# An encoder layer with seven-product weight blocks: two of the four sums of quarters of the weights are added by accumulating transfers

## The chip, the core and the metric

The kernel runs on one core of a Trainium2 chip. The metric is the device time of one execution in microseconds, taken as the median of several runs; a profiled execution gives the trace that the rows below come from. Engines are named as the profile names them: PE (TensorE matmul) and PEld (its weight load), DVE (VectorE), ACT (ScalarE), POOL (GpSimd) and SP (SyncE, which here only issues transfers).

## What is computed

One layer of an encoder on 528 tokens (16 learned ones and 512 of the input) with 1024 features, all in float32. A SwiGLU half-step, a mixer (a gated linear recurrence beside a Fourier mixing), a second SwiGLU half-step and a last norm follow each other. The half-steps are where the change sits:

```python
def swiglu(h, w_in, w_out):
    gate, up = jnp.split(h @ w_in, 2, axis=-1)
    return (jax.nn.silu(gate) * up) @ w_out

h = h + 0.5 * swiglu(rms_norm(h, norm_ffn1[l]), w_ffn1_in[l], w_ffn1_out[l])   # w_in 1024 x 5632, w_out 2816 x 1024
...
h = h + 0.5 * swiglu(rms_norm(h, norm_ffn2[l]), w_ffn2_in[l], w_ffn2_out[l])
return rms_norm(h, norm_final)[:, N_META:]
```

## The kernel before

**Exact parts.** Every float32 operand of a product is split into a rounded part `hi` and a rest `lo`, and a product is three matmuls (hi by hi, hi by lo, lo by hi, in `mm3`). For weights, `split_w` takes the `hi` part on ACT (L87) and the `lo` part on DVE (L88).

**Seven products in place of eight.** The 2816 hidden features are done in 22 blocks of 128. A block needs a gate and an up product over 1024 features. The first blocks of a half-step (4 of the first, 2 of the second) are done plainly; the other 38, here called *pairs* 0 to 37 (0 to 17 in the first half-step, 18 to 37 in the second), treat gate and up as a 2 by 2 matrix of quarters [A11 A12; A21 A22] (rows gate and up, columns the two halves of the features) and the stream, split by features and tokens, likewise, and need seven products of quarters. PE does them in the order p1 (A11), p2 (A12), p6 (S2), p5 (S1), p7 (S3), p3 (S4), p4 (A22). The tiles for that are made in three jobs:

- `pair_blocks`: loads the two raw tiles of 512 KB (`g`, then `u`, L101), splits all of the first (*A*, L87 and L88) and the second half of the second (`jh`, `jl`), then adds in place on DVE: S3 = A11 - A21 (L110), S1 = A21 + A22 (L111), S2 = A22 - S3 (L112).
- `pair_sums`: splits S1 and S2 (*S*, one L87 and one L88 of 1024 columns), then S4 = A12 - S2 (L120).
- `pair_differences`: splits S3 and S4 (*D*).

The stream's side has matching sums (`sums_of_x`), and `pair` puts the seven products together on DVE, multiplies by the norm's roots, takes Silu on ACT and splits the result.

**Order.** Weight jobs stand in one list in the order of their use, and `block` starts a job three jobs ahead of its use (LOOK = 3). Raw tiles share four buffers and split tiles four, so a load waits until an earlier split has read its buffer. A tile scheduler fixes the order on each engine when the program is built; on the chip each engine runs its list strictly in order. With chunks of four blocks (pairs 7 to 17 in the first half-step), each pair is followed on PE by two blocks of the way out (`po`, L462 takes them up). There the load of the tile that is split first waits for the *S* split of the pair before, and the load of the other for its *D* split.

Of the kernel before, what the change touches and what calls it, by code (L numbers as in the profile page):

```python
# [12 lines left out]
ALU = mybir.AluOpType  # L13
# [49 lines left out]
def encoder_layer(ctx: ExitStack, tc: tile.TileContext, xT, vecs, w1i, w1o, wm, wg, wo, w2i, w2o,  # L63
# [13 lines left out]
    def spans(n):  # L77
        """The pieces of n columns that fit in a bank."""
        return [(0, n)] if n <= 512 else [(0, n // 2), (n // 2, n)]
# [5 lines left out]
    # [A11 A12; A21 A22]: rows gate and up, columns the two halves of the features  # L85
# [9 lines left out]

    def pair_blocks(pair):
        """A11, A12 and A22; then, in place, S3 = A11 - A21, S1 = A21 + A22 and S2 = A22 - S3."""
        raw = []
        for src in pair["src"]:
            r = wraw.tile([P, 1024], F32, tag="raw", name="raw")  # L100
            nc.sync.dma_start(r.rearrange("p (k m) -> p k m", m=P), src)  # L101
            raw.append(r)
        pair["raw"] = raw
        hi, lo = w_tiles()
        split_w(hi, lo, raw[0])
        jh = state["pool"].tile([P, 512], F32R, tag="jh", name="jh")
        jl = state["pool"].tile([P, 512], F32R, tag="jl", name="jl")
        split_w(jh, jl, raw[1][:, 512:])
        g, u = raw
        nc.vector.tensor_tensor(g[:, :512], g[:, :512], u[:, :512], op=ALU.subtract)  # L110
        nc.vector.tensor_tensor(u[:, :512], u[:, :512], u[:, 512:], op=ALU.add)  # L111
        nc.vector.tensor_tensor(u[:, 512:], u[:, 512:], g[:, :512], op=ALU.subtract)  # L112
        return [(quarter(hi, 0), quarter(lo, 0)), (quarter(hi, 1), quarter(lo, 1)), (quarter(jh, 0), quarter(jl, 0))]

    def pair_sums(pair):
        """S1 and S2; then, in place, S4 = A12 - S2."""
        g, u = pair["raw"]
        hi, lo = w_tiles()
        split_w(hi, lo, u)
        nc.vector.tensor_tensor(g[:, 512:], g[:, 512:], u[:, 512:], op=ALU.subtract)  # L120
        return [(quarter(hi, 0), quarter(lo, 0)), (quarter(hi, 1), quarter(lo, 1))]

    def pair_differences(pair):
        """S3 and S4."""
        g = pair.pop("raw")[0]
        hi, lo = w_tiles()
        split_w(hi, lo, g)
        return [(quarter(hi, 0), quarter(lo, 0)), (quarter(hi, 1), quarter(lo, 1))]

    def parts_given(src):  # L130
        """Both parts of a table, as they come."""
        parts = []
        for i, t in enumerate(w_tiles()):
            raw = wraw.tile([P, 1024], F32, tag="raw", name="raw")
            t, raw = [x[:, :3 * HT] for x in (t, raw)]
            nc.sync.dma_start(raw.rearrange("p (k m) -> p k m", m=HT), src[i])
            nc.scalar.activation(t, raw, AF.Copy)
            parts.append(t.rearrange("p (k m) -> p k m", m=HT))
        return parts

# [1 line left out]
    # (source, partitions, tiles, columns of a tile, tiles per load) or a part of a pair  # L142
    jobs = []

    def ffn_steps(chunks, late):
        """Blocks of features on their way in, each followed by its share of the preceding chunk's way out."""
        steps, f0, prev = [], 0, None
        for c in chunks:
            for i in range(c):
                steps.append(("in", f0 + i, None))  # L150
                if prev:
                    steps += [("out", prev, d) for d in range(*(max(0, ND - (c - k) * ND // c - late) if k < c else ND for k in (i, i + 1)))]
            prev = (f0, f0 + c)
            f0 += c
        return steps + [("out", prev, d) for d in range(ND)]
# [3 lines left out]
    def ffn_jobs(wi, wo_, steps, classic):  # L159
        for kind, f, d in steps:  # L160
            if kind == "out":
                jobs.append((wo_[d][:, f[0]:f[1], :], P, f[1] - f[0], P, 8))
            elif f in classic:
                for b in range(2):
                    jobs.append((wi[f, b], P, 8, P, 2 if len(jobs) < 3 else 8))
            else:
                pair = {"src": (wi[f, 0], wi[f, 1])}
                for part in (pair_blocks, pair_sums, pair_differences):
                    jobs.append((part, pair))
# [56 lines left out]
    def mm3(outs, wh, wl, xh, xl, first, last):  # L226
        """outs[i] += w.T @ x[i], w and x in two exact parts each."""
        for i, o in enumerate(outs):
            nc.tensor.matmul(o, wh, xh[i], start=first, stop=False)  # L229
        for i, o in enumerate(outs):  # L230
            nc.tensor.matmul(o, wh, xl[i], start=False, stop=False)  # L231
        for i, o in enumerate(outs):
            nc.tensor.matmul(o, wl, xh[i], start=False, stop=last)  # L233

    def halves(t, n):
        """The first n columns of a tile by their pieces."""
        return [t[:, a:b] for a, b in spans(n)]

    def times(out_, ps, r, n):
        """out = ps * r, with ps in banks."""  # L240
# [12 lines left out]
    def vec(name, i=0):  # L253
        return V[:, VOFF[name] + i: VOFF[name] + i + 1]

# [11 lines left out]
    # the tensor engine's clock rises while these run, ahead of the first loads' landing  # L267
# [4 lines left out]
    def split_to(hi, lo, src, scale=None):  # L272
        """hi + lo = src * scale exactly but for float32's own rounding."""
# [13 lines left out]
    # [B11 B12; B21 B22]: rows the two halves of the features, columns those of the tokens.  # L287
    # T1 = B12 - B11, T2 = B22 - T1, T3 = T2 - B11, -T4 = B21 - T2, one tile of the features at a time
    def sums_of_x(g, t0, n, k):
# [6 lines left out]
        nc.vector.scalar_tensor_tensor(t1, a[:, m:], vec(g, k), xg[:, :m], op0=ALU.mult, op1=ALU.subtract)  # L296
        nc.vector.scalar_tensor_tensor(t2, b[:, m:], vec(g, k + 4), t1, op0=ALU.mult, op1=ALU.subtract)
        nc.vector.tensor_tensor(t3, t2, xg[:, :m], op=ALU.subtract)
        nc.vector.scalar_tensor_tensor(t4, b[:, :m], vec(g, k + 4), t2, op0=ALU.mult, op1=ALU.subtract)
# [13 lines left out]
    # 1 / sqrt(mean + eps) of each token: the roots are taken with tokens on partitions, then spread to all partitions  # L313
# [20 lines left out]
    def spread_in(ps, q, m):  # L334
        """ps[:, t] = q of token t on all partitions."""
# [14 lines left out]
    def ffn(X, XT, ss, t0, n, steps, classic, on_done, tail, lead=None):  # L350
        st = {"R": ss} if lead else {}
        half = n // 2
        with tc.tile_pool(name="ffn", bufs=10) as fp, tc.tile_pool(name="ffnt", bufs=2) as ft:
# [19 lines left out]
            def pair(R):  # L373
                """Gate and up of one block of features, from seven products of quarters."""
# [10 lines left out]
                gv, uv = q[:, :2, :half], u[:, :, :half]  # L385
# [21 lines left out]
                nc.scalar.activation(gv, gv, AF.Silu)  # L407
# [58 lines left out]
    # softplus(-lambda) = max(-lambda, 0) + log1p(exp(-|lambda|))  # L466
# [21 lines left out]
    # only sets with the root and without it follow: the root's is at hand when the first norm is due  # L488
    nc.scalar.activation(s2[:, :1], epsc, AF.Sqrt)

# [44 lines left out]
    # [cos W | sin W] of each group  # L535
# [11 lines left out]
    X2, XT2 = [], []  # L547
    ss2 = new_ss()
    with tc.tile_pool(name="mx", bufs=1) as mx, tc.tile_pool(name="mt", bufs=2) as mt:
# [5 lines left out]
        def projecting(t0):  # L555
            """One block of the projection, a tile of the features at a time."""
# [7 lines left out]
        def project():  # L564
            """One block of the projection, with steps of what is under way between its products."""
# [4 lines left out]
        # recurrence inputs: depthwise convolution  # L570
# [42 lines left out]
        # Fourier mixing over the tokens t = 0..T-1: s, d[t] = v[t] + v[t + T/2], v[t] - v[t + T/2] give the even and  # L613
        # the odd outputs; the cosines multiply s[t] + s[T/2 - t] and d[t] - d[T/2 - t], the sines the other two, t = 0..T/4
# [19 lines left out]
        # with r in a = exp(-8 r sp) and t = tanh(4 r sp): sqrt(1 - a^2) = (1 + a) sqrt(t)  # L634
# [3 lines left out]
        def recurrences():  # L638
            """The recurrences in steps, each table of the scalar engine's once."""
# [52 lines left out]
        def features(s):  # L692
            """Step s of the token tiles: their transform over the features, tokens on partitions."""
# [34 lines left out]
        def tokens(s, A, py):  # L728
            """Step s of the sum over the tokens."""
# [90 lines left out]
    def tail(acts, ft):  # L820
# [15 lines left out]
        def residual(d0, d1, t0, t1, ps, sq):  # L836
            """The stream's last values, their squares, and the values times the last norm's gain."""
# [4 lines left out]
        def group(t0, t1, between):  # L842
            """The stream's last values for a group of tokens, and the roots of their mean squares."""
# [49 lines left out]
        def finishing(q, t0, t1, queues):  # L893
            """The steps from the roots to the end of a group."""
# [99 lines left out]
```

## Time and profile before

| | us |
|---|---|
| median of 3 runs (lowest to highest) | 883.19 (883.08 to 883.46) |
| span of the profiled execution, first to last instruction | 880.1 |
| difference of the two | 3.1 |
| PE busy in the span | 867.3 |
| DVE busy | 751.8 |
| ACT busy | 423.8 |
| POOL busy | 0.2 |

The span is what the trace shows; the 3.1 us are what the runs' median has beside it. A busy time is the union of an engine's instructions. An engine at 99% can still not be made faster by work taken from another, and one at 85% can still be waited for, so what counts is who waits where.

### The profile page before, as it was taken

To read this page: it belongs to the slowest core of one execution; us is meant where nothing else is said; L and a number is where in the kernel's file an instruction comes from. 1 tells how busy PE (TensorE), PEld (TensorE's weight loads), DVE (VectorE), ACT (ScalarE), POOL (GpSimd) and SP (SyncE) were. 2 spreads that over 40 slices of the span, in tenths; PEclk is the share of its full clock that TensorE was granted. 3 is DMA by queue.
4 is the path that set the end of the run, shared out by engine and by line. 5 is a ranking of instruction groups with operands and counts; after the bars stand their busy time and mean duration, and the time that the engine had idled before them with its cause. 6 is when DMAs were issued, how large, how long until landed. Compare 5 with 4: busy or idle time off the path is not lost.

```text
span 880.1 us, 15868 instructions
## 1 busy us (share of the span) xinstructions
PE 867.3 (99%) x6410; PEld 826.8 (94%) x6410; DVE 751.8 (85%) x1280; ACT 423.8 (48%) x625; POOL 0.2 (0%) x4
## 2 busy tenths in 40 slices
PE   9999999999999999999999999999999999999996
PEld 8999999999999999999887888999899999999996
DVE  7999987898898896867998689999999888789864
ACT  7644433344344343667837555444444444334354
POOL 0000000000000000000000000000000000000000
PEclk9999999999999999999999999999999999999998
DMA  7423333324323223423412331223343324323312
GB/s 236 149 64 112 86 108 96 96 73 122 95 90 118 83 85 109 147 67 107 135 47 96 93 99 48 85 85 120 98 131 81 115 79 120 112 73 101 99 54 96
DMA packets 33497, 88.15 MB, mean 100 GB/s; under 512 B 3728, under 2 KB 7568, under 8 KB 33424
## 3 DMA queue, kind: packets, MB, share of 16 engines
q1 hardware_dynamic: 32880, 86.62, 32.4%
q8 instruction: 50, 0.82, 0.4%
q10 hardware_dynamic: 544, 0.52, 0.2%
q14 instruction: 23, 0.19, 0.1%
HBM read 85.03 MB, written 2.10 MB: 99 GB/s over the span
## 4 chain that ended last, share of the span: by engine, by line
PE 93%; DVE 4%; ACT 1%; DMA 0%; issue 0%; SPq 0%; DVEq 0%
PE pp L229 15%; PE pp L233 15%; PE pp L231 14%; PE po L233 9%; PE po L231 9%; PE po L229 9%; PE pw L231 2%; PE pw L233 2%; PE pm L229 2%; PE pm L233 2%; PE pm L231 2%; PE pw L229 2%; PE pu L229 1%; PE pu L231 1%; PE pu L233 1%; PE pg L229 1%
## 5 line engine op out<-in xcount | busy, mean ns | idle before, releaser
L87 ACT ACTIVATE whi<-raw 128x1024 fp32r<-128x1024 f32 x114 | 120.1, 1060 | 190.0 <-DVE raw L112 130.4
L88 DVE TENSOR_TENSOR wlo<-raw,whi 128x1024 fp32r<-128x1024 f32 x114 | 138.7, 1218 | 13.7 <-ACT whi L87 13.3
L229 PE MATMUL pp<-th,whi 128*128 128x256 f32 (+1 forms) x456 | 129.2, 283 | 0.0
L233 PE MATMUL pp<-th,wlo 128*128 128x256 f32 (+1 forms) x456 | 128.9, 283 | 0.0
L233 PE MATMUL pp<-xh,wlo 128*128 128x256 f32 (+1 forms) x456 | 128.9, 283 | 0.0
L231 PE MATMUL pp<-xl,whi 128*128 128x256 f32 (+1 forms) x456 | 128.8, 283 | 0.0
L229 PE MATMUL pp<-xh,whi 128*128 128x256 f32 (+1 forms) x456 | 128.6, 282 | 0.0
L233 PE MATMUL po<-ah,wlo 128*128 128x264 f32 (+1 forms) x496 | 128.3, 317 | 0.0
L231 PE MATMUL pp<-tl,whi 128*128 128x256 f32 (+1 forms) x456 | 128.3, 281 | 0.0
L231 PE MATMUL po<-al,whi 128*128 128x264 f32 (+1 forms) x496 | 128.2, 316 | 0.0
L229 PE MATMUL po<-ah,whi 128*128 128x264 f32 (+1 forms) x496 | 128.1, 316 | 0.0
L211 ACT ACTIVATE whi<-raw 128x512 fp32r<-128x512 f32 (+4 forms) x120 | 88.1, 739 | 81.7 <-PE pp L231 26.6
L212 DVE TENSOR_TENSOR wlo<-raw,whi 128x512 fp32r<-128x512 f32 (+4 forms) x120 | 98.3, 823 | 13.9 <-ACT whi L211 12.1
L233 PEld LDWEIGHTS po<-ah,wlo 128*128 128x128 f32 x496 | 81.4, 188 | 6.4
L231 PEld LDWEIGHTS po<-al,whi 128*128 128x128 f32 x496 | 81.7, 188 | 5.8
L229 PEld LDWEIGHTS po<-ah,whi 128*128 128x128 f32 x496 | 81.5, 188 | 5.7
L229 PEld LDWEIGHTS pp<-xh,whi 128*128 128x128 f32 x456 | 85.9, 188 | 0.8
L231 PEld LDWEIGHTS pp<-xl,whi 128*128 128x128 f32 x456 | 85.8, 188 | 0.8
L231 PEld LDWEIGHTS pp<-tl,whi 128*128 128x128 f32 x456 | 85.9, 188 | 0.0
L233 PEld LDWEIGHTS pp<-xh,wlo 128*128 128x128 f32 x456 | 85.8, 188 | 0.0
L233 PEld LDWEIGHTS pp<-th,wlo 128*128 128x128 f32 x456 | 85.8, 188 | 0.0
L229 PEld LDWEIGHTS pp<-th,whi 128*128 128x128 f32 x456 | 85.7, 188 | 0.0
(219 smaller groups left out, 1769.0 us busy)
## 6 DMA issues: line engine op xcount, KB each, us to landing
raw<-in_w2i SPq DMA_DIRECT2D x44, 512.0 KB, 3.6
raw<-in_w1i SPq DMA_DIRECT2D x41, 512.0 KB, 3.6
raw<-in_w1o SPq DMA_DIRECT2D x32, 256.0 KB, 2.9
raw<-in_wm SPq DMA_DIRECT2D x12, 512.0 KB, 3.6
raw<-in_w2o SPq DMA_DIRECT2D x24, 256.0 KB, 2.8
raw<-in_w2o SPq DMA_DIRECT2D x16, 320.0 KB, 3.0
raw<-in_wo SPq DMA_DIRECT2D x8, 512.0 KB, 3.6
raw<-in_w1o SPq DMA_DIRECT2D x8, 384.0 KB, 3.2
```

Of the source, the lines that this page charges most:

```text
L87: nc.scalar.activation(hi, raw, AF.Copy)
L88: nc.vector.tensor_tensor(lo, raw, hi.bitcast(F32), op=ALU.subtract)
L211: nc.scalar.activation(hi[:p, s], raw[:p, s], AF.Copy)
L212: nc.vector.tensor_tensor(lo[:p, s], raw[:p, s], hi[:p, s].bitcast(F32), op=ALU.subtract)
L229: nc.tensor.matmul(o, wh, xh[i], start=first, stop=False)
L231: nc.tensor.matmul(o, wh, xl[i], start=False, stop=False)
L233: nc.tensor.matmul(o, wl, xh[i], start=False, stop=last)
```

## The change

Two of the three sums in `pair_blocks` are no longer added by DVE: POOL issues two transfers of 256 KB that read a quarter of the weights from HBM a second time and add it to the raw tile where it lies (`accum_op`). A transfer can add but not subtract, so signs are turned: the two source blocks are swapped, four of the stream's sums are negated, gate and up change their tiles in `pair`, and Silu takes its input with a factor of -1. The two sums left to DVE are additions. A small tile of negated gains is made once.

```diff
@@ pair_blocks
-        g, u = raw
-        nc.vector.tensor_tensor(g[:, :512], g[:, :512], u[:, :512], op=ALU.subtract)
-        nc.vector.tensor_tensor(u[:, :512], u[:, :512], u[:, 512:], op=ALU.add)
-        nc.vector.tensor_tensor(u[:, 512:], u[:, 512:], g[:, :512], op=ALU.subtract)
+        u, g = raw
+        src = pair["src"][1]
+        nc.gpsimd.dma_start(quarter(g, 0), src[:, 4:, :], accum_op=ALU.add)
+        nc.gpsimd.dma_start(quarter(u, 0), src[:, :4, :], accum_op=ALU.add)
+        nc.vector.tensor_tensor(g[:, 512:], g[:, 512:], u[:, :512], op=ALU.add)
@@ pair_sums, pair_differences
-        g, u = pair["raw"]
+        u, g = pair["raw"]
+        hi, lo = w_tiles()
+        split_w(hi, lo, g)
+        nc.vector.tensor_tensor(u[:, 512:], u[:, 512:], g[:, 512:], op=ALU.add)
+        return [(quarter(hi, 0), quarter(lo, 0)), (quarter(hi, 1), quarter(lo, 1))]
+
+    def pair_differences(pair):
+
+        u = pair.pop("raw")[0]
         hi, lo = w_tiles()
         split_w(hi, lo, u)
-        nc.vector.tensor_tensor(g[:, 512:], g[:, 512:], u[:, 512:], op=ALU.subtract)
...
@@ ffn_jobs
-                pair = {"src": (wi[f, 0], wi[f, 1])}
+                pair = {"src": (wi[f, 1], wi[f, 0])}
@@ sums_of_x
-        nc.vector.scalar_tensor_tensor(t1, a[:, m:], vec(g, k), xg[:, :m], op0=ALU.mult, op1=ALU.subtract)
-        nc.vector.scalar_tensor_tensor(t2, b[:, m:], vec(g, k + 4), t1, op0=ALU.mult, op1=ALU.subtract)
-        nc.vector.tensor_tensor(t3, t2, xg[:, :m], op=ALU.subtract)
-        nc.vector.scalar_tensor_tensor(t4, b[:, :m], vec(g, k + 4), t2, op0=ALU.mult, op1=ALU.subtract)
+        nc.vector.scalar_tensor_tensor(t1, a[:, m:], less(g, k), xg[:, :m], op0=ALU.mult, op1=ALU.add)
+        nc.vector.scalar_tensor_tensor(t2, b[:, m:], less(g, k + 4), t1, op0=ALU.mult, op1=ALU.subtract)
+        nc.vector.scalar_tensor_tensor(t3, t2, -1.0, xg[:, :m], op0=ALU.mult, op1=ALU.subtract)
+        nc.vector.scalar_tensor_tensor(t4, b[:, :m], less(g, k + 4), t2, op0=ALU.mult, op1=ALU.subtract)
@@ pair
-                gv, uv = q[:, :2, :half], u[:, :, :half]
+                uv, gv = q[:, :2, :half], u[:, :, :half]
...
-                nc.scalar.activation(gv, gv, AF.Silu)
+                nc.scalar.activation(gv, gv, AF.Silu, scale=-1.0)
@@ encoder_layer
+    nc.vector.tensor_scalar(minus, V[:, :24], -1.0, None, op0=ALU.mult)
```

What the built program makes of it is shown at pair 9, in the stretch of chunks of four. DVE, before, from the *A* split of pair 9 on (L399 to L404 gather the products of pair 8; `raw_2437` and `raw_2439` are the pair's raw tiles):

```order
L88 TENSOR_TENSOR wlo_2442<-raw_2437,whi_2441 128x1024 [waits DMAHW3_49,Activation_49]
L399 TENSOR_TENSOR q_2367<-q_2367,pp_2452 128x264 [waits PE_49]
L110 TENSOR_TENSOR raw_2437<-raw_2437,raw_2439 128x512 [waits DVE_49]
L400 TENSOR_TENSOR u_2368<-q_2367,pp_2423 128x264 [waits DVE_49]
L111 TENSOR_TENSOR raw_2439<-raw_2439 128x512 [waits DVE_49]
L402 TENSOR_TENSOR q_2367<-u_2368,pp_2467 128x264 [waits PE_49]
L112 TENSOR_TENSOR raw_2439<-raw_2439,raw_2437 128x512 [waits DVE_49]
L404 TENSOR_TENSOR u_2368<-q_2367,pp_2481 128x264 [waits DVE_49,PE_49]
L406 TENSOR_TENSOR q_2367<-q_2367,r1_385 128x528
L120 TENSOR_TENSOR raw_2437<-raw_2437,raw_2439 128x512 [waits DVE_49]
L88 TENSOR_TENSOR wlo_2506<-raw_2439,whi_2505 128x1024 [waits Activation_49]
L408 TENSOR_TENSOR q_2367<-q_2367,r1_385 128x528 [waits Activation_49]
```

DVE, with the change, the same place (`raw_2439` and `raw_2441` are now the raw tiles; L407 to L412 gather the products, L414 is the old L406, L122 the old L120, and `DMASW` is the semaphore of a transfer that POOL issued):

```order
L88 TENSOR_TENSOR wlo_2444<-raw_2439,whi_2443 128x1024 [waits DMAHW3_49,Activation_49]
L407 TENSOR_TENSOR q_2369<-q_2369,pp_2454 128x264 [waits PE_49]
L408 TENSOR_TENSOR u_2370<-q_2369,pp_2425 128x264 [waits DVE_49]
L410 TENSOR_TENSOR q_2369<-u_2370,pp_2469 128x264 [waits PE_49]
L412 TENSOR_TENSOR u_2370<-q_2369,pp_2483 128x264 [waits DVE_49,PE_49]
L114 TENSOR_TENSOR raw_2441<-raw_2441,raw_2439 128x512 [waits DMASW3_49]
L414 TENSOR_TENSOR u_2370<-u_2370,r1_387 128x528 [waits DVE_49]
L122 TENSOR_TENSOR raw_2439<-raw_2439,raw_2441 128x512 [waits DVE_49]
L88 TENSOR_TENSOR wlo_2508<-raw_2441,whi_2507 128x1024 [waits DMASW2_49,Activation_49]
L416 TENSOR_TENSOR u_2370<-u_2370,r1_387 128x528 [waits Activation_49]
L470 SCALAR_TENSOR_TENSOR hall_80<-po_2505,hall_80 128x264 [waits PE_49]
L417 TENSOR_TENSOR q_2369<-q_2369,u_2370 128x528 [waits DVE_49]
```

The two sums are gone from between the gathering instructions, and the third (L112, now L114) stands behind all of them and waits for a transfer. POOL, where there was nothing before, now has these rows for pairs 9 and 10:

```order
L112 DMA raw_2441<-in_w1i 128x512 [waits DMAHW4_49,DMASW1_49,DVE_49]
L113 DMA raw_2439<-in_w1i 128x512 [waits DMAHW3_49,DMASW0_49,DVE_49]
L112 DMA raw_2642<-in_w1i 128x512 [waits DMAHW0_49,DMASW3_49,DVE_49]
L113 DMA raw_2640<-in_w1i 128x512 [waits DMAHW7_49,DMASW2_49,DVE_49]
```

L113 is the one that L114 waits for, and the DVE event that L113 itself waits for is the end of the *A* split of its pair, since it writes over the quarter that this split reads. ACT keeps the order that it had (with the change, at pair 9; L415 is Silu):

```order
L87 ACTIVATE jh_2447<-raw_2441 128x512 [waits DMAHW4_49]
L87 ACTIVATE whi_2443<-raw_2439 128x1024 [waits DMAHW3_49,PE_49,Activation_49]
L87 ACTIVATE whi_2507<-raw_2441 128x1024 [waits DVE_49,DMASW2_49,PE_49,Activation_49]
L415 ACTIVATE u_2370<-u_2370 128x528 [waits DVE_49]
L87 ACTIVATE whi_2540<-raw_2439 128x1024 [waits DVE_49,DMASW3_49,PE_49,Activation_49]
```

Only waits on a transfer of POOL's are new here. SP's list and, but for one group of four small matmuls that stands three matmuls earlier, PE's are as they were; the mixer's lists are the same on DVE, ACT and PE.

## Rows read from the trace of the kernel before

**Rows 1.** The page: span, busy time of each engine, the chain's shares by engine

```profile
span 880.1 us, 15868 instructions
...
PE 867.3 (99%) x6410; PEld 826.8 (94%) x6410; DVE 751.8 (85%) x1280; ACT 423.8 (48%) x625; POOL 0.2 (0%) x4
...
PE 93%; DVE 4%; ACT 1%; DMA 0%; issue 0%; SPq 0%; DVEq 0%
```

**Rows 2.** Windows: stretch, its length, busy time of each engine, granted clock

```profile
core 0: us, PE busy (x) PEld busy (x) DVE busy (x) ACT busy (x) POOL busy (x), PEclk, DMA share, GB/s
70.00:340.00 270.00, 270.00 (x2226) 270.00 (x2225) 234.60 (x407) 108.22 (x146) 0.00 (x0) 1.00 0.33 97
545.00:850.00 305.00, 305.00 (x2155) 285.41 (x2154) 272.25 (x448) 127.68 (x178) 0.00 (x0) 1.00 0.34 99
416.00:475.00 59.00, 55.29 (x369) 49.71 (x368) 51.96 (x86) 36.00 (x60) 0.00 (x0) 0.97 0.29 95
```

**Rows 3.** Groups by line on DVE: busy time, mean ns of one

```profile
L110 DVE TENSOR_TENSOR raw<-raw 128x512 f32<-128x512 f32 x38 | 26.0, 684 | 0.0
...
L404 DVE TENSOR_TENSOR u<-q,pp 128x256 f32<-128x256 f32 (+1 forms) x38 | 15.8, 416 | 0.2
```

**Rows 4.** Timeline of PE: p1 of pairs 8 and 9, p7 of pair 9

```profile
183.78 0.28 PE L229 MATMUL pp<-xh,whi 128*128 128x264 f32 x1
...
199.81 0.28 PE L229 MATMUL pp<-xh,whi 128*128 128x264 f32 x1
...
205.63 0.28 PE L229 MATMUL pp<-th,whi 128*128 128x264 f32 x1
```

**Rows 5.** Timeline of DVE: D of pair 8; A, L112, S and D of pair 9

```profile
183.37 1.21 DVE L88 TENSOR_TENSOR wlo<-raw,whi 128x1024 fp32r<-128x1024 f32 x1
...
190.82 1.22 DVE L88 TENSOR_TENSOR wlo<-raw,whi 128x1024 fp32r<-128x1024 f32 x1 [0.59 <-ACT whi L87]
...
194.18 0.68 DVE L112 TENSOR_TENSOR raw<-raw 128x512 f32<-128x512 f32 x1
...
196.34 1.21 DVE L88 TENSOR_TENSOR wlo<-raw,whi 128x1024 fp32r<-128x1024 f32 x1
...
199.40 1.21 DVE L88 TENSOR_TENSOR wlo<-raw,whi 128x1024 fp32r<-128x1024 f32 x1
```

**Rows 6.** Timeline of SP and ACT: pair 9's second load, its jh, A and S

```profile
184.61 0.33 SPq L101 DMA_DIRECT2D raw<-in_w1i  x1
...
188.22 0.63 ACT L87 ACTIVATE jh<-raw 128x512 fp32r<-128x512 f32 x1 [0.76 <-DMA raw<-in_w1i]
189.72 1.06 ACT L87 ACTIVATE whi<-raw 128x1024 fp32r<-128x1024 f32 x1 [0.87 <-PE pp L231]
194.98 1.06 ACT L87 ACTIVATE whi<-raw 128x1024 fp32r<-128x1024 f32 x1 [4.20 <-DVE raw L112]
```

**Rows 7.** DMA issues: size of one, median us from issue to landing

```profile
raw<-in_w1i SPq DMA_DIRECT2D x41, 512.0 KB, 3.6
raw<-in_w1o SPq DMA_DIRECT2D x32, 256.0 KB, 2.9
...
wfc<-in_fw SPq DMA_DIRECT2D x1, 256.0 KB, 2.5
```

**Rows 8.** Second half-step: window of pairs 21 to 25; S of pair 21; its p6

```profile
565.53:637.83 72.30, 72.30 (x519) 67.87 (x517) 68.69 (x118) 30.65 (x43) 0.00 (x0) 1.00 0.34 106
...
576.62 1.22 DVE L88 TENSOR_TENSOR wlo<-raw,whi 128x1024 fp32r<-128x1024 f32 x1
...
581.14 0.28 PE L229 MATMUL pp<-th,whi 128*128 128x256 f32 x1
```

**Rows 9.** Windows at two waits of PE in the mixer

```profile
438.44:440.64 2.20, 0.29 (x4) 0.07 (x2) 2.20 (x5) 0.21 (x1) 0.00 (x0) 1.00 0.50 140
441.04:444.45 3.41, 3.41 (x21) 3.31 (x21) 3.35 (x7) 1.12 (x3) 0.00 (x0) 0.50 0.19 76
456.80:458.29 1.49, 0.40 (x3) 0.03 (x1) 1.46 (x3) 1.47 (x3) 0.00 (x0) 1.00 0.77 239
```

More of the change, by code (lines that the diff above doesn't have):

```diff
@@ L108, in pair_blocks @@
         split_w(jh, jl, raw[1][:, 512:])
-        g, u = raw
-        nc.vector.tensor_tensor(g[:, :512], g[:, :512], u[:, :512], op=ALU.subtract)
-        nc.vector.tensor_tensor(u[:, :512], u[:, :512], u[:, 512:], op=ALU.add)
-        nc.vector.tensor_tensor(u[:, 512:], u[:, 512:], g[:, :512], op=ALU.subtract)
+        u, g = raw
[3 more added lines that the diff above has]
+        nc.vector.tensor_tensor(g[:, 512:], g[:, 512:], u[:, :512], op=ALU.add)
         return [(quarter(hi, 0), quarter(lo, 0)), (quarter(hi, 1), quarter(lo, 1)), (quarter(jh, 0), quarter(jl, 0))]
     def pair_sums(pair):
-        g, u = pair["raw"]
+        u, g = pair["raw"]
[5 more added lines that the diff above has]
+        u = pair.pop("raw")[0]
         hi, lo = w_tiles()
         split_w(hi, lo, u)
-        nc.vector.tensor_tensor(g[:, 512:], g[:, 512:], u[:, 512:], op=ALU.subtract)
[L121 to L127, printed above, removed]
         return [(quarter(hi, 0), quarter(lo, 0)), (quarter(hi, 1), quarter(lo, 1))]
@@ L254, in vec, with less @@
         return V[:, VOFF[name] + i: VOFF[name] + i + 1]
+    minus = const.tile([P, 24], F32, name="minus")
+    def less(name, i):
+        return minus[:, VOFF[name] + i: VOFF[name] + i + 1]
     hall = xs.tile([P, ND, T], F32, tag="h", name="hall")
```

## Prediction

> **What bounds the kernel now.** I read the page first. PE is busy in 867.3 of 880.1 us and holds 93% of the chain that ended last; DVE has 85% of the span, but 4% of the chain [rows 1]. Then the windows of the two half-steps, where all the pairs are: PE is busy in 270.00 of 270.00 us and in 305.00 of 305.00 us at the full granted clock, and only the mixer has gaps, 59.00 less 55.29 us [rows 2]. The reader is to see that in the half-steps PE never waits: no work taken from DVE there can shorten the time, however busy DVE is. What it can do is the other thing: come too late for PE. So I read, pair by pair, how early each split tile is ready and which waits tie one pair to the next.
>
> **What is removed.** L110 and L111 take 38 x 0.68 us each, 52 us of DVE [rows 3]. None of it is on PE's path, so it is worth 0.
>
> **What is added: a wait in a closed loop.** With the change, L114 (the old L112) waits for a transfer that can be issued only when the *A* split has ended. Call the time from the end of *A* to the start of L114 X. Take pair 9, and p1 of pair 8 at 183.78 and of pair 9 at 199.81, so that PE needs 16.03 us for a pair with its two blocks of the way out; p7, which needs *D*, begins 5.82 us after p1 [rows 4].
>
> First the loop, step by step, with nothing but its own waits:
> - *D* of pair 8 ends at 183.37 + 1.21 = 184.58 [rows 5]. The second load of pair 9 waits for it, is issued at 184.61, and `jh` starts on the landed tile at 188.22 [rows 6]: 3.64 us.
> - `jh` 0.63, then *A*'s part on ACT 1.06 [rows 6] (it stands behind `jh` in ACT's list), then DVE's part: it began 0.04 after ACT's end and took 1.22 [rows 5, 6], 1.26. From the end of *D* to the end of *A*: 6.6 us.
> - X.
> - From L112 to the end of *D*: 194.18 to 199.40 + 1.21 = 200.61, 6.43 us [rows 5]. The changed list has one gathering instruction (L404, 0.42 [rows 3]) less in this place, but *S* then comes so early that it waits a little for its part on ACT; I take 6.2.
>
> The loop takes 6.6 + X + 6.2 = 12.8 + X. While X is under 16.03 - 12.8 = 3.23, PE's own pace holds and nothing is seen. Above that, each pair comes X - 3.23 later than the one before. Before, the same loop had the sums in X's place (L112 began 2.14 us after the end of *A* [rows 5]) and 0.87 us in which ACT waited for PE [rows 6]: it was closed with under 1 us to spare, which the shares of busy time don't show.
>
> How much may be eaten up first: while *A* is held by PE, as now, it ends 190.82 + 1.22 - 183.78 = 8.26 us after p1 of the pair before, so *D* of pair 9 ends at 198.24 + X, against p7 at 205.63: 7.39 - X to spare. That is so in pair 7, the first of the chunks of four; ten more follow to pair 17. Their lateness at the end, all of it time that PE waits, is 10 (X - 3.23) - (7.39 - X) = 11 X - 39.7 us, and nothing up to X = 3.6. Pairs 3 to 6 come with three blocks of the way out, a longer beat, and are safe.
>
> In the second half-step the blocks of the way out are spread unevenly, and I count DVE as a whole. Over five pairs (20 to 24, in which the weights of 21 to 25 are made) it is busy in 68.69 of 72.30 us [rows 8]. The change takes 5 x 1.37 off and adds at L114 what is left of X after the four or five gathering instructions between *A* and L114 (by the order, 1.3 to 1.9 us, mean 1.65): 68.69 - 6.8 + 5 (X - 1.65) = 53.6 + 5 X. *S* of pair 21 ends at 577.84, p6 that needs it begins at 581.14 [rows 8], 3.3 us to spare. So PE waits from 53.6 + 5 X = 75.6 on, X = 4.4, and then 5 us for each us of X.
>
> **X itself** is the number that the trace lacks: POOL issues no transfer before. Below, it can't be shorter than the quickest load of the same 256 KB, 2.5 us, and 2.9 is the median in the half-steps [rows 7]; both are SP's issue with nothing added. By bytes, a transfer that adds has to read its destination too, 256 + 256 KB, as much as a 512 KB load: 3.6 us [rows 7]. Above, if reading and adding went one after the other, 2 x 2.9 = 5.8. I take 4.3, the middle of 2.9 and 5.8, which is 0.7 over the 512 KB row for an issue by POOL's software and the hand-over from DVE. It is nearer to 3.6 than to 5.8 because all the engines' queues are two thirds idle here (share 0.33 [rows 2]). Ends kept for the range: 2.5 and 5.8.
>
> The Trainium skill, page "DMA: Bandwidth & Descriptors", section "Anatomy of one DMA", fits a transfer issued by GpSimd as 2.0 us and its bytes at 436 GB/s: 2.6 us for 256 KB, an estimate by which the loop stays inside PE's beat and the change costs nothing. No run here shows such a transfer. The page "Collectives: The Full Stack", section "The bandwidth ceiling", says that a transfer that adds needs two source reads and so runs at half the rate; that speaks for more than 2.6.
>
> **The rest at nothing.** The two transfers of a pair add 38 x 2 x 256 KB, 20 MB beside DMA engines that are one third busy. POOL's first transfer of a pair has its load and the *D* split before it long behind it and is done before the second is due. The negated gains (one small DVE instruction) lie under the first loads; the turned signs replace instructions by others of the same size; the gate path now needs p4's sum, but its first instruction stood behind p4's before as well. The mixer's lists are unchanged.
>
> **Sum.** 11 x 4.3 - 39.7 = 7.6 us in the first half-step, 0 in the second: the profiled span goes from 880.1 to 887.7, and with the 3.1 us beside it the median from 883.2 to 890.8.
>
> **Rivals.**
> - *Hidden anyway.* X up to 3.75: 11 X - 39.7 is under 1.6, no change, 883 to 885. For it: the 2.5 and 2.9 us rows. Against it: these are plain loads issued by SP. It decides at X = 3.6. Chance 0.30. The rule on 2.6 us above is this case.
> - *Read and add in turn.* X of 5.2 to 5.8: 17.5 to 24.1 us in the first half-step and 4 to 7 in the second, 905 to 914. Chance 0.12.
> - *The clock falls too.* After a wait of 2.20 us in the mixer a stretch of 3.41 us was granted 0.50, the lower of the clock's two levels (1.2 and 2.4 GHz); a wait of 1.49 us stands at the full level [rows 9]. A stall of X - 3.23 reaches 2.2 at X = 5.4; then each late pair loses some 1.7 us more, about 8 pairs, 14 us: 920 to 928. Chance 0.04.
> - *Faster.* The mixer's gaps (3.7 us) and its 3.41 us at half clock (1.7) are all there is to win, 877.8. They are DVE's doing [rows 2], but no pair lies there and its lists are as before. Chance 0.04.
>
> **Chances.** X from 3.75 to 5.2, slower by 2 to 22 us: 0.50, the likeliest; its own range is 885 to 905. With the rivals: faster by over 0.2% (1.8 us, about what a measurement of this kernel can tell) 0.04, within 0.30, slower 0.66. The range goes from no change, 882.5, to X = 5.6 (21.9 + 6), 911.
>
> **What the changed profile would show.** If right: DVE about 700 us busy; L114 as the line before which DVE idles longest, ended by the transfer; X near 4.3; PE with waits at p6 or p7, ended by the *S* or *D* split, some 1 us each, in the later pairs of the first half-step, from pair 10 or 11, and next to none in the second half-step. The beat of those pairs would be 17.1 in place of 16.03. If X is under 3.6, PE is full in both windows and the time is the old one. Wrong in its mechanism I would be if PE waits at p1 or for a PSUM bank that L470 frees late, or if the waits lie in the second half-step while the first is full: then it is DVE as a whole, not the loop. A transfer that is slow because DVE's work keeps POOL from issuing it would show as an X that varies with what DVE does.

## The result and the profile after

The changed kernel takes 915.93 us (median of 4 runs, 914.22 to 918.32) against 883.13 us before: ratio 1.0385, 95% interval 1.0369 to 1.0400. It is slower, as forecast, by 33 us and not by 8, and it lies above the range given.

The page of the profiled execution: the span, the busy time of each engine, the shares of the chain that ended last, and the group of the last addition (busy time, mean ns of one, idle time of DVE before it and what ended most of it):

```profile
span 916.5 us, 16093 instructions
...
PE 882.1 (96%) x6410; PEld 831.2 (91%) x6410; DVE 708.8 (77%) x1205; ACT 410.5 (45%) x625; POOL 66.1 (7%) x80
...
PE 40%; DMA 24%; DVE 24%; issue 6%; ACT 5%; DVEq 0%; POOL 0%; ACTq 0%; POOLq 0%; SPq 0%
...
L114 DVE TENSOR_TENSOR raw<-raw 128x512 f32<-128x512 f32 x38 | 26.3, 693 | 93.9 <-DMA raw<-in_w1i 48.2
```

DVE lost 43 us of busy time, from 751.8 to 708.8. That is less than the 52 us counted from the lengths of the two sums, because neighbouring records overlap and the busy time is their union (`jl` of pair 9 below is 0.69 us long, and the next record starts 0.60 us after it). As forecast, DVE now idles before L114, 93.9 us in all, and transfers end that. The chain was 93% PE [rows 1], and now it runs more through transfers and DVE than through PE. The windows of the two half-steps and the mixer (columns as in [rows 2]):

```profile
70.00:340.00 270.00, 262.48 (x2116) 258.49 (x2116) 205.22 (x357) 94.58 (x137) 26.75 (x31) 1.00 0.51 123
416.00:475.00 59.00, 54.00 (x400) 50.13 (x399) 53.54 (x93) 39.24 (x66) 0.00 (x0) 1.00 0.32 100
545.00:850.00 305.00, 293.00 (x1994) 267.77 (x1993) 236.22 (x381) 116.46 (x165) 30.26 (x35) 1.00 0.51 120
```

Read the counts here, not only the busy time. The records of matmuls overlap: in the wait of pair 9 shown below the matmul that waits starts 0.99 us after the one before it, where the step is otherwise 0.12, so 0.87 us are lost and only 0.71 show as idle time. But 2116 matmuls were issued in 270 us where 2226 were before, and 1994 in 305 where there were 2155. At the mean step before (0.121 and 0.142 us) that is some 13 and 23 us of missing work, an estimate, since the delay shifts other matmuls into a window; the starts of p1 below are the better measure. Both half-steps wait, at the full granted clock.

Pair 9, beside [rows 4 to 6], on DVE (*D* of pair 8; `jl`, *A*, L114, *S* and *D* of pair 9), then on POOL, then on PE:

```profile
194.32 1.22 DVE L88 TENSOR_TENSOR wlo<-raw,whi 128x1024 fp32r<-128x1024 f32 x1
...
199.78 0.69 DVE L88 TENSOR_TENSOR jl<-raw,jh 128x512 fp32r<-128x512 f32 x1 [1.06 <-ACT jh L87]
200.38 0.42 DVE L404 TENSOR_TENSOR u<-q,pp 128x264 f32<-128x264 f32 x1
200.72 1.23 DVE L88 TENSOR_TENSOR wlo<-raw,whi 128x1024 fp32r<-128x1024 f32 x1
...
206.48 0.69 DVE L114 TENSOR_TENSOR raw<-raw 128x512 f32<-128x512 f32 x1 [2.85 <-DMA raw<-in_w1i]
...
208.43 1.23 DVE L88 TENSOR_TENSOR wlo<-raw,whi 128x1024 fp32r<-128x1024 f32 x1
...
211.49 1.22 DVE L88 TENSOR_TENSOR wlo<-raw,whi 128x1024 fp32r<-128x1024 f32 x1
```

```profile
199.64 0.86 POOL L112 DMA_DIRECT2D raw<-in_w1i  x1 [13.21 <-DMA raw<-in_w1i]
202.25 0.86 POOL L113 DMA_DIRECT2D raw<-in_w1i  x1 [1.74 <-DVE wlo L88]
```

```profile
208.72 0.28 PE L233 MATMUL pp<-tl,whi 128*128 128x264 f32 x1
209.71 0.39 PE L235 MATMUL pp<-th,wlo 128*128 128x264 f32 x1 [0.71 <-DVE wlo L88]
```

*A* ends at 201.95, POOL issues the late transfer 0.30 us after that, L114 starts at 206.48: X = 4.53. From *D* to *D* it is 17.17 us, where PE alone needs 16.03. *S* ends at 209.66, and PE, at p6, goes on at 209.71. That is the wait that was forecast, at its place and in its size. What was not foreseen is where else it stands. The median X is 4.22 in pairs 8 to 17 and 4.30 in pairs 21 to 37, and in 30 of the 38 pairs PE waits at p6 for the DVE part of *S*. Taking the start of p1 in each pair against before, PE has come 14.3 us late by pair 18 (559.77 against 545.60, and 0.17 early at pair 0), and another 19.4 us by pair 37 (860.73 against 827.13); the other 2.8 of the 36.4 us between the two spans lie behind that, some 1.7 of them in 3.4 us from 894.5 us on at a granted clock of 0.50, a stretch that the kernel before does not have.

The chain that ended last, in the second half-step, from *D* of pair 24 to *D* of pair 26 (start, length, what):

```profile
647.63 3.79 DMA raw<-in_w2i
...
653.13 1.16 DVE wlo L88
...
654.58 3.92 DMA raw<-in_w2i
...
658.52 0.70 DVE raw L114
...
660.55 1.17 DVE wlo L88
...
661.73 4.86 DMA raw<-in_w2i
...
668.23 1.24 DVE wlo L88
...
669.75 4.05 DMA raw<-in_w2i
...
677.33 1.15 DVE wlo L88
...
678.50 4.75 DMA raw<-in_w2i
```

No PE stands in it. It is the closed loop of the first half-step, laid over two pairs: the second load of pair 25 waits for *D* of pair 24, *A* for the load, the late transfer for *A*, *S* for the transfer; then the second load of pair 26 waits for *S* of pair 25, and so on. It takes 678.50 - 647.63 = 30.87 us. From p1 of pair 24 to p1 of pair 26 PE took 29.01 us before.

### The profile page after: what moved, and what is told of

Same layout as the page of the kernel before. It is cut to its first block, busy times and chain, and to the rows that moved or that the text cites. A ratio compares the mean times of both kernels' runs of the same rounds, so it can differ in the third digit from the quotient of the medians.

```text
span 916.5 us, 16093 instructions
## 1 busy us (share of the span) xinstructions
PE 882.1 (96%) x6410; PEld 831.2 (91%) x6410; DVE 708.8 (77%) x1205; ACT 410.5 (45%) x625; POOL 66.1 (7%) x80
## 3 DMA queue, kind: packets, MB, share of 16 engines
q0 software_dynamic: 10944, 19.93, 14.3%
## 4 chain that ended last, share of the span: by engine, by line
PE 40%; DMA 24%; DVE 24%; issue 6%; ACT 5%; DVEq 0%; POOL 0%; ACTq 0%; POOLq 0%; SPq 0%
DMA raw<-in_w2i 15%; DVE wlo L88 10%; DMA raw<-in_w1i 8%; PE pp L235 3%; PE pp L231 3%; PE po L231 3%; PE pp L233 3%; ACT whi L87 3%; PE po L233 3%; PE po L235 3%; DVE raw L114 2%; PE pw L233 2%; DVE u L416 2%; PE pw L235 2%; PE pm L231 2%
## 5 line engine op out<-in xcount | busy, mean ns | idle before, releaser
L87 ACT ACTIVATE whi<-raw 128x1024 fp32r<-128x1024 f32 x114 | 118.0, 1051 | 182.5 <-DVE raw L114 131.3
L235 PE MATMUL pp<-th,wlo 128*128 128x256 f32 (+1 forms) x456 | 133.6, 293 | 16.4 <-DVE wlo L88 16.4
L114 DVE TENSOR_TENSOR raw<-raw 128x512 f32<-128x512 f32 x38 | 26.3, 693 | 93.9 <-DMA raw<-in_w1i 48.2
```

What stands on the lines that cost most here:

```text
L87: nc.scalar.activation(hi, raw, AF.Copy)
L114: nc.vector.tensor_tensor(g[:, 512:], g[:, 512:], u[:, :512], op=ALU.add)
```

## The experiments

Theory 1, from here on *the loop*: the added time is what the loop through a raw tile's release, its load, *A*, the late transfer, and *S* or *D* exceeds PE's beat by, in both half-steps. Theory 2, *the traffic*: 20 MB more hold up the loads. Theory 3, as predicted, for the second half-step: there DVE's work as a whole decides.

All in one table. X is the median from the end of *A* to the last addition's start (L114), in pairs 8 to 17 and 21 to 37. Lateness is the start of p1 against the kernel before, gained from pair 0 to 18 and from 18 to 37.

| run | time, us | ratio to before, 95% | X, us | lateness, us |
|---|---|---|---|---|
| changed kernel | 915.93 | 1.0369 to 1.0400 | 4.22, 4.30 | 14.3, 19.4 |
| all_dve | 881.56 | 0.9987 to 1.0005 | 2.14, 2.12 | -0.1, 0.0 |
| early_only | 882.08 | 0.9994 to 1.0013 | 1.20, 1.18 | 0.0, 0.0 |
| late_only | 920.69 | 1.0416 to 1.0455 | 4.27, 4.21 | 14.1, 21.7 |
| late_second | 905.47 | 1.0244 to 1.0283 | 2.14, 4.25 | 0.0, 22.1 |
| from8 | 887.55 | 1.0042 to 1.0076 | 4.29, 2.11 | 5.9, 0.0 |
| plain | 882.84 | 0.9998 to 1.0018 | 3.13, 3.13 | 0.0, 0.0 |
| half_late | 889.95 | 1.0076 to 1.0108 | 3.31, 3.41 | 0.2, 7.1 |
| two_issues | 928.78 | 1.0506 to 1.0544 | 4.57, 4.60 | 19.3, 24.5 |
| a_first | 899.64 | 1.0175 to 1.0209 | 5.60, 5.38 | 5.2, 11.0 |
| a_first_late | 901.69 | 1.0209 to 1.0246 | 4.27, 4.18 | 7.0, 11.2 |
| a_first_s1 | 883.97 | 1.0012 to 1.0035 | 4.21, 4.30 | 0.0, 2.4 |
| raw5 | 898.31 | 1.0168 to 1.0204 | 4.45, 4.81 | 0.7, 15.2 |

### Which part of the change

all_dve keeps the turned signs and does all sums on DVE; early_only and late_only give one of the two to POOL; late_second gives POOL the late one in the second half-step alone, and from8 gives it both in pairs 8 to 17 alone.

```diff
-        nc.gpsimd.dma_start(quarter(g, 0), src[:, 4:, :], accum_op=ALU.add)
-        nc.gpsimd.dma_start(quarter(u, 0), src[:, :4, :], accum_op=ALU.add)
+        if pair["late"]:        # all_dve: never; late_only: always; late_second: w2i; from8: f >= 12 of w1i
+            nc.gpsimd.dma_start(quarter(u, 0), src[:, :4, :], accum_op=ALU.add)
+        else:
+            nc.vector.tensor_tensor(u[:, :512], u[:, :512], g[:, :512], op=ALU.add)
+        nc.vector.tensor_tensor(g[:, :512], g[:, :512], g[:, 512:], op=ALU.add)
```

In from8 the pairs named keep the changed kernel's two transfers; in early_only the second transfer alone becomes an addition (of `g[:, 512:]`).

> The changed signs and sources kept, all four sums by VectorE. Theory 1 (a closed loop: a pair's second load waits for a split of the pair before, and the late transfer's time X of about 4.3 us from the end of the A split to L114 lies in it): no X beyond the sums, so the time of before, 881 to 885 us. Theory 2 (the added 20 MB hold up the loads): no transfers, so 881 to 885 too. If the turned signs or the other order of sources cost something, it shows here alone: over 885.

> Only the early transfer (S1, into the gate tile) by POOL; the sum that waits for the A split is VectorE's, and reads the other quarter of the gate tile (as if it were the first), so the values are others and the work is the same. Theory 1: nothing of the transfer is in the loop, 881 to 885 us. Theory 2 (traffic): half of the added bytes, so half of the loss, about 899 us.

> Only the late transfer (into the up tile, behind the A split) by POOL; S1 is VectorE's, in the idle time ahead of L114. Theory 1: X stays near 4.2 us and with it nearly all of the loss, 908 to 917 us, and PE waits at p6 in most pairs. Theory 2: half of the bytes, about 899 us, and X shorter.

> The late transfer by POOL in the second half-step alone; all other sums by VectorE. It tells the two readings of the second half-step apart. As predicted (VectorE's work as a whole decides there, PE waits from X = 4.4 on): X about 4.2 us, and 881 to 884 us. The loop through raw tiles, A and the transfer (in the changed kernel it took 30.9 us for two pairs where PE needs 29.0): 19 us and more of loss in the second half-step alone, 900 to 906 us, with PE full in the first.

> Both transfers by POOL in pairs 8 to 17 of the first half-step alone, as the changed kernel has them; all other sums by VectorE. It tests the sum of the prediction where its starting point holds: before pair 8 nothing has been eaten up, so D of pair 8 has 7.39 - X = 3.1 us to spare at X = 4.27, and each of the pairs 9 to 17 comes X - 3.23 = 1.04 us later than the one before. By this: 9 x 1.04 - 3.1 = 6.2 us of PE's waiting, the first of it in pair 11 or 12, and 887 to 889 us in all. If instead the lateness of the changed kernel's first half-step (14 us) came from the pairs 8 to 17 themselves (a first transfer that finds no slack, a slope that is steeper), 893 us or more.

The signs cost nothing. Half of the traffic, 10 MB and 38 instructions of POOL, costs nothing either when nothing waits for it in the loop: early_only is at 882.08. With plain below, which has all 20 MB and takes 882.84, the traffic is out. All of the loss is the late transfer's. late_only's median is even above the changed kernel's and above the 908 to 917 expected. Its S1 sum stands ahead of `jl` and *A* in DVE's list, so from *D* to the end of *A* it takes 6.82 us in pairs 9 to 17 and not 6.44, and the loop 17.30 and not 16.98; and in its profiled execution the granted clock was 0.50 for 3.4 us at 850 us, some 1.7 us more. That these make the difference is not shown: the two profiled executions have nearly the same span, 916.3 and 916.5 us.

late_second settles the second half-step: 22.1 us of lateness arise there with no transfer of POOL's ahead of it (some 1.7 of them in 3.4 us at a granted clock of 0.50, from 819.9 us on), and this while DVE is less busy than before. The window, as above; before, DVE was busy in 272.25 us of it [rows 2]:

```profile
545.00:850.00 305.00, 290.81 (x2004) 267.84 (x2003) 242.23 (x395) 111.65 (x159) 16.44 (x19) 0.99 0.41 108
```

So theory 3 falls: no engine is short of time there; it is the loop. from8 shows that the sum of the prediction holds where its starting point does: 6.2 us expected, 5.9 measured, with PE's first wait at p6 of pair 11 (at 234 us), as it says:

```profile
70.00:234.00 164.00, 164.00 (x1354) 164.00 (x1353) 131.82 (x226) 61.87 (x85) 7.07 (x8) 1.00 0.39 105
234.00:340.00 106.00, 103.09 (x827) 101.10 (x826) 82.82 (x147) 39.45 (x60) 10.38 (x12) 1.00 0.51 122
```

### What X is made of

plain drops `accum_op`, so both transfers overwrite; half_late gives POOL 128 KB of the late one; two_issues cuts it into two of 128 KB.

```diff
-        nc.gpsimd.dma_start(quarter(u, 0), src[:, :4, :], accum_op=ALU.add)
+        nc.gpsimd.dma_start(quarter(u, 0)[:, :2, :], src[:, :2, :], accum_op=ALU.add)
+        nc.vector.tensor_tensor(u[:, 256:512], u[:, 256:512], g[:, 768:], op=ALU.add)   # half_late
+        nc.gpsimd.dma_start(quarter(u, 0)[:, 2:, :], src[:, 2:4, :], accum_op=ALU.add)  # two_issues
```

> Both of POOL's transfers without the addition: they overwrite their quarter (the sums are left out), with the same waits, bytes and places. If adding costs the transfer nothing, X stays at 4.3 us and the time at 914 to 918 us, and the 4.0 us of a transfer are those of one that POOL issues; if the addition is a large part (a second read), X falls to about 3.4 and the time to 883 to 890 us. I expect a small fall, X of 4.0 and 905 to 912 us.

> The changed kernel with half of the late transfer (128 KB) left to POOL; VectorE adds the other 256 columns, from another quarter (values are others, the work is the same). Theory 1: each us of X is worth some 28 us of time over 30 late pairs, so the time tells X: if the transfer's time went with its bytes (0.86 us of issue, some 3 us for 256 KB) X would be 2.8 us and the time 883 to 886; if it is mostly fixed, X is about 3.9 and the time 902 to 908 us. I expect the second. Theory 2 (traffic): three quarters of the bytes, 907 us whatever X is.

> The changed kernel with the late transfer cut into two of 128 KB, the same bytes, one more issue of 0.86 us by POOL. Theory 1: X is longer by 0.5 to 0.9 us, and the time by 14 to 25 us: 930 to 941 us. Theory 2 (traffic): the same bytes, so 916 us.

DMA issues (count, size, median us from issue to landing), of the changed kernel, of plain, and of half_late:

```profile
raw<-in_w2i POOLq DMA_DIRECT2D x40, 256.0 KB, 4.0
raw<-in_w1i POOLq DMA_DIRECT2D x36, 256.0 KB, 4.0
```

```profile
raw<-in_w2i POOLq DMA_DIRECT2D x40, 256.0 KB, 3.0
raw<-in_w1i POOLq DMA_DIRECT2D x36, 256.0 KB, 3.0
```

```profile
raw<-in_w2i POOLq DMA_DIRECT2D x20, 128.0 KB, 3.1
raw<-in_w1i POOLq DMA_DIRECT2D x18, 128.0 KB, 3.0
```

A transfer that POOL issues without adding takes 3.0 us, next to nothing over SP's 2.9 [rows 7]. The addition makes it 4.0. These medians are over early and late transfers together; for the 38 late ones alone they are 2.8 and 4.0, and X falls from 4.22 and 4.30 to 3.13, so that the addition costs the late transfer 1.1 to 1.2 us. That is the whole of the result: at X = 3.13 PE is full in both half-steps and the time is that of before, with the same waits, bytes and queue. The windows of plain:

```profile
70.00:340.00 270.00, 270.00 (x2226) 270.00 (x2225) 217.91 (x375) 105.10 (x146) 16.09 (x30) 1.00 0.42 127
545.00:850.00 305.00, 305.00 (x2158) 285.55 (x2157) 254.26 (x409) 127.02 (x179) 19.85 (x37) 1.00 0.43 129
```

plain was expected at 905 to 912, and missed by more than 20 us because the addition is dearer than I thought. half_late was expected at 902 to 908 and came to 890: half of the bytes, added, take 1 us less. two_issues came out just under its 930 to 941. X grew by only 0.3 us, since the halves run side by side (the first takes 3.1 us, the second, issued 0.5 us later, 3.7), and the time by 13.

The column X beside the lateness gives the threshold. In pairs 8 to 17 of the changed kernel the loop without X takes 16.98 - 4.3 = 12.7 us, so it meets PE's 16.04 at X = 3.3: plain (3.13) is free, half_late (3.31) stands just at it. In the second half-step the two X in the 30.87 us are 4.24 and 4.37; without them 22.3 are left, and 29.01 are met at X = 3.4: plain is free, half_late (3.41) loses 7 us.

### Opening the loop with X left as it is

a_first puts *A*'s part on ACT ahead of `jh`, so that *A* need not wait for the pair's second load. a_first_late gives S1 back to DVE in addition, and a_first_s1 also orders that sum behind *A* on DVE. raw5 has five raw tiles (and 9 activation buffers for 10, to make room).

```diff
-        split_w(hi, lo, raw[0])
+        first = nc.scalar.activation(hi, raw[0], AF.Copy)
+        low = nc.vector.tensor_tensor(lo, raw[0], hi.bitcast(F32), op=ALU.subtract)
...
+        then = nc.scalar.activation(jh, raw[1][:, 512:], AF.Copy)
+        tc.add_manual_dep(then.ins, first.ins.name, ...)
...
-        nc.gpsimd.dma_start(quarter(g, 0), src[:, 4:, :], accum_op=ALU.add)
+        s1 = nc.vector.tensor_tensor(g[:, :512], g[:, :512], g[:, 512:], op=ALU.add)
+        tc.add_manual_dep(s1.ins, low.ins.name, ...)
```

> The changed kernel with one order added: on ScalarE the A split's part stands ahead of jh, so A waits for the pair's first load alone, which is issued about 3 us before the second. Both transfers stay. Theory 1: 3 us or more come out of the loop, it needs about 14 us where PE needs 16.03, and the time falls to 882 to 888 us with X still over 4 us. Theory 2 and a theory that POOL's transfers are slow as such: the bytes and the transfers are the same, so 910 us or more.

> As a_first (A split ahead of jh on ScalarE), and the early transfer is taken back to VectorE, so that the late one has POOL's queue to itself. In a_first the two were issued within 0.6 us of each other and X rose from 4.3 to 5 and 6.5 us, and 17 us of loss stayed. Theory 1 (loop): with X back at about 4.2 us the loop needs some 13.5 us in the first half-step, under PE's 16.03, and 882 to 890 us result; what is left stands in the second half-step. Rival (a transfer that adds slows everything near it, whatever waits for it): half of the transfers, so half of a_first's loss, about 891 us, and spread over both half-steps.

> As a_first_late, but with the S1 sum on VectorE ordered behind the A split. In a_first_late that sum stood ahead of A in VectorE's list and reads the second load's tile, so A waited for the second load after all (A ended 2.8 us after jh's start in the first half-step, as before the reorder). Theory 1: now A waits for the first load alone, X stays near 4.2, the loop needs some 13.5 us: 881 to 887 us. Rival (any transfer that adds costs about 18 us whatever the order): 895 us or more.

> The changed kernel with five raw tiles in place of four (room for it comes from one activation buffer less, 9 of 10, which may cost something of its own). By the program the second load of a pair of the chunks of four then waits for the S split of the pair before and not for D, which ends 3.05 us later; in the second half-step the loads of every other pair wait for no split of a pair at all. The transfers, their bytes and X (4.2 to 4.3 us) stay. Theory 1 (the loop is closed by the raw tiles): some 17.0 - 3.05 = 13.9 us for the loop, under PE's 16.03, so 881 to 887 us. Rival (the transfer's own lateness at S, or the traffic, without a loop): no change, 912 us or more.

a_first brought back half, where 882 to 888 were expected. Its X had grown; at pair 13 POOL issues both transfers within a microsecond, and L117 (the old L114) waits 3.46 us:

```profile
258.41 0.86 POOL L115 DMA_DIRECT2D raw<-in_w1i  x1 [15.60 <-DVE u L407]
259.38 0.86 POOL L116 DMA_DIRECT2D raw<-in_w1i  x1
```

```profile
257.86 1.22 DVE L107 TENSOR_TENSOR wlo<-raw,whi 128x1024 fp32r<-128x1024 f32 x1
...
264.82 0.69 DVE L117 TENSOR_TENSOR raw<-raw 128x512 f32<-128x512 f32 x1 [3.46 <-DMA raw<-in_w1i]
```

From the issue of the late one to L117 it is 5.4 us in place of 4.0: the two hold each other up, and what the order gained X took back in part. a_first_late missed its 882 to 890: X was back at 4.27, but at pair 9 the S1 sum, which reads the second load's tile, stands ahead of *A* on DVE (194.25, *A* at 195.73), so *A* waited for that load all the same. With that one order mended, a_first_s1 takes 883.97 us with X at 4.21 and 4.30, the same transfer that costs 33 us in the changed kernel. Pair 9 of it on DVE, and the windows:

```profile
190.15 1.23 DVE L107 TENSOR_TENSOR wlo<-raw,whi 128x1024 fp32r<-128x1024 f32 x1 [0.59 <-ACT whi L106]
191.29 0.69 DVE L112 TENSOR_TENSOR jl<-raw,jh 128x512 fp32r<-128x512 f32 x1
191.89 0.69 DVE L116 TENSOR_TENSOR raw<-raw 128x512 f32<-128x512 f32 x1
...
195.59 0.69 DVE L118 TENSOR_TENSOR raw<-raw 128x512 f32<-128x512 f32 x1 [1.34 <-DMA raw<-in_w1i]
```

```profile
70.00:340.00 270.00, 270.00 (x2226) 270.00 (x2224) 227.38 (x395) 103.19 (x147) 13.41 (x16) 1.00 0.42 114
545.00:850.00 305.00, 303.42 (x2137) 283.30 (x2136) 262.20 (x428) 122.00 (x177) 16.43 (x19) 1.00 0.43 115
```

PE is full again in the first half-step; 2.4 us of lateness are left, in pairs 21 to 23. It does not beat the kernel before, and by [rows 2] nothing that only frees DVE can: PE has no wait to give back in the half-steps.

raw5 is a half miss, with 898 where 881 to 887 were expected. By its program the second load now waits for *S* instead of *D*, and the first half-step is free at X = 4.45 (0.7 us, 270.00 of 270.00 us busy): what closes the loop is the raw tile's release. The second half-step still lost 15.2 us, 6.8 of them at one place, pair 30, whose *A* ends at 716.23. POOL's rows, and PE's wait that follows and the stretch after it (windows, as above):

```profile
713.01 0.88 POOL L112 DMA_DIRECT2D raw<-in_w2i  x1 [11.66 <-DMA raw<-in_w2o]
720.95 0.88 POOL L112 DMA_DIRECT2D raw<-in_w2i  x1 [7.06 <-DMA raw<-in_w2i]
721.53 1.19 POOL L113 DMA_DIRECT2D raw<-in_w2i  x1
```

```profile
724.96:728.75 3.79, 0.28 (x3) 0.07 (x2) 1.89 (x4) 1.06 (x1) 0.00 (x0) 0.87 0.26 46
727.80:734.60 6.80, 5.39 (x23) 5.09 (x24) 6.80 (x10) 4.39 (x6) 0.00 (x0) 0.50 0.18 52
```

The early transfer of pair 31 stands ahead of the late one of pair 30 in POOL's list and waits for a load until 720.4 (a slow one: it landed 6.1 us after its issue, where the median of such a load is 3.6 [rows 7]); the late one, ready since 716.23, is issued at 721.53. In a list that is worked off in order a transfer is late for whatever stands before it. PE then goes 3.79 us with next to nothing to do, and the granted clock is 0.50 in the 6.80 us from 727.8 on; half of these, some 3.4 us, are the clock's share in what pair 30 lost. The other 8 us of raw5 are not taken apart, nor is what the missing activation buffer costs.

## Why the prediction was wrong

- **The bound before, and what is removed: right.** 43 us less of DVE's work, nothing gained; all_dve and plain have the time of before at different DVE loads (751.8 and 713.5 us busy).
- **X: right in its value, wrong in its make-up.** Taken 4.3, measured 4.22 and 4.30; 4.3 was the middle of two wide bounds, so that it fits is in good part luck. I put 0.7 us down to POOL's issue and the hand-over and the rest to twice the bytes. It is 0.30 of hand-over (from the end of *A* to POOL's issue, in 36 of 38 pairs), 2.8 for the late transfer as POOL issues it, and 1.2 for the addition. The Trainium skill, page "DMA: Bandwidth & Descriptors", section "Anatomy of one DMA", fits a transfer that GpSimd issues as 2.0 us and its bytes at 436 GB/s, which is 2.6 us for 256 KB, an estimate; the trace has a median of 2.8 without the addition (3.0 over both transfers), and the consequence drawn from it, no loss, is what plain shows. The Trainium skill, page "Collectives: The Full Stack", section "The bandwidth ceiling", gives a ReduceScatter half the rate of an AllGather because its add needs two source reads; carried over to this transfer, which the page does not do, that would be 0.6 us more for 256 KB, an estimate from the two pages; measured is 1.2.
- **The loop and its threshold, pairs 8 to 17: right.** Taken 12.8 + X against 16.03, threshold 3.23; measured 12.7 and 16.04, 3.3; the mean beat of pairs 9 to 17 came to 16.9, 17.1 was forecast. from8, which meets the starting point of the sum, lost 5.9 us where the sum gives 6.2.
- **The start of the sum failed: "Pairs 3 to 6 come with three blocks of the way out, a longer beat, and are safe."** Their beat is longer, 18.9 us, but so is their loop: the splits of those blocks stand ahead of *A* on ACT and on DVE (at pair 4 one of 0.83 and one of 0.95 us), so that 8.3 to 9.2 us lie between *D* and the end of *A*, not 6.6, and with X and 6.1 to 6.4 us after it the loop takes 18.9 to 19.8. The four to six microseconds that PE had in hand at *S* of pairs 1 to 3 were gone by pair 3. At pair 7, where I counted 3.1 us to spare, *D* ended when PE was already at p7, and the loop of 19.7 us there (X was 5.58 in this pair, the transfer itself slow) fell on a beat of 16.03: 3.4 us at once. So 14.3 us for the first half-step, not 7.6. That the slack was lost there is shown by from8; how the parts of it add up is read from the trace alone. By it, with no slack left, 11 (4.22 - 3.23) = 10.9 us come from the pairs 7 to 17, 1.9 had come before pair 7, and 1.4 are the slow transfer of pair 7, an estimate of 14.2 in all.
- **The step that failed most: "In the second half-step the blocks of the way out are spread unevenly, and I count DVE as a whole."** It gave 0 at X = 4.3, with a threshold of 4.4; measured are 19.4 us, and late_second shows 22.1 without any in the first half-step. A loop of waits needs no busy engine: DVE was 77% busy there, and over both half-steps it had 2.5 us of idle time at each L114 (94 us in 38). By the loop over two pairs the threshold was 3.4 in place of 4.4. That the loads of these pairs wait for *S* or *D* just as in the first half-step stood in the program; I followed the loop where the pattern was regular and replaced it by an average where it was not.
- **Taken at nothing.** The traffic: right, by plain. That the early transfer is done before the late one is due: wrong, at pair 9 it lands at 203.64, 1.4 us after the late one's issue. It costs nothing that shows: X is the same in late_only, which has no early transfer (4.27 and 4.21).
- **The rivals.** Hidden anyway: no, X was 1 us too long. Read and add in turn: no, X of 5.2 to 5.8 was not met; its 905 to 914 us are nearer to the time than the sum, but from a loss that it puts mostly in the first half-step. The clock: it stayed at 1.00 in both windows of the changed kernel (above). Of the other runs, late_only, late_second and two_issues had one stretch at 0.50 among the pairs of the second half-step, of 3.4 us, some 1.7 us each, and raw5 one of 6.8.

## What to carry to other kernels

Slack is not what the shares of busy time leave over, but what the tightest cycle of waits leaves over (buffer freed, loaded, split, transferred, split, freed): before taking work off a busy engine by adding a transfer, write that cycle down in every stretch where its period differs, irregular ones too, and add the new latency to it. If the latency must be there, take other waits out of the cycle (order the work that needs only the first load ahead of the work that needs the second), and look at what an in-order list puts ahead of the one instruction that the cycle runs through. And a late start is not forgiven: where the loop is as long as the beat, no slack grows back.

## What was not expected of the hardware

- The addition costs a 256 KB transfer 1.0 us (median 4.0 against 3.0; 1.2 for the late ones, 4.0 against 2.8), while its issue by POOL costs next to nothing against SP's (3.0 and 2.9). Of transfers that add, one of 128 KB takes 3.0 to 3.1 (half_late), and of two that follow each other the second takes 3.7 (two_issues); 256 KB take some 5.4 us when another was issued one microsecond earlier (pair 13 of a_first).
- Single transfers of the same kind stray: X was 5.58 in pair 7 of the changed kernel, with no load of SP's issued between 165.1 and 175.8 us, while pairs 8 to 17 lie between 4.03 and 4.53. What makes it stray is open.
- In the mixer of the changed kernel a wait of PE of 2.21 us was not followed by a fall of the granted clock, though before the same wait of 2.20 us was [rows 9]. The same wait stands in all runs; the fall came in some of them (all_dve, early_only, a_first) and not in others (plain, a_first_s1, late_only). Columns as there:

```profile
452.69:454.90 2.21, 0.29 (x4) 0.08 (x2) 2.21 (x5) 0.22 (x1) 0.00 (x0) 1.00 0.69 180
455.00:475.00 20.00, 17.60 (x128) 15.67 (x129) 19.78 (x30) 7.22 (x15) 0.00 (x0) 1.00 0.13 44
```
